# A pooled subtraction in tiles of six rows: the first tile of three rows (2 and 1), the last of five (3, 1 and 1)

## The chip, the cores and the metric

The kernel runs on one core of a Trainium2 chip. The metric is the device time of one execution in microseconds (us); the time of a kernel is the median of its runs. The profile comes from one further execution, in which the hardware profiler recorded instructions and DMA packets.

## The reference

The input `x` is a float32 tensor of shape (8, 64, 256, 256), 134.22 MB. Each 256x256 image is cut into windows of 8x8. The maximum of each window is taken, spread back over its window, and subtracted from the input:

```python
x_r = x.reshape(B, C, oH, 8, oW, 8)
pooled = x_r.max(axis=(3, 5))
upsampled = np.repeat(np.repeat(pooled, 8, axis=2), 8, axis=3)
return x - upsampled
```

The output has the shape and type of the input. Every byte is read once and written once, 268.44 MB in all.

## The kernel before, in words

Eight image lines of 256 values make one "row" of 2048 floats (8 KB), which holds 32 whole windows. There are 16384 such rows. A tile gives each of the 128 partitions R consecutive rows, so a tile of R rows is R MiB. The rows are cut into 22 tiles: tile 0 of `sum(HEAD)` = 4 rows, tiles 1 to 20 of `SIZE` = 6 rows, and tile 21 of `sum(TAIL)` = 4 rows. Together these are 4 + 120 + 4 = 128 rows per partition.

One buffer in SBUF, `ring`, has four slots of six rows each (`SLOTS`, line 15). Tile i lives in slot (i - 1) modulo 4: tiles 1, 2, 3 in slots 0, 1, 2, tile 0 in slot 3, tile 4 in slot 3 again, and so on; tile 21 is in slot 0 with tile 17 before it. The data are changed in place: a tile is loaded into its slot, reduced into `tops`, subtracted in the slot, and stored from there. Nothing is copied.

Three engines' queues share the work, each in an order that is written out by hand:

- SP issues the loads (line 113). Tile 0 is loaded in the pieces of `HEAD`, every other tile in one transfer. Before a load into a slot that was used, SP waits (line 110) until the stores of the tile before it in that slot have landed; so SP issues tiles 0 to 3 at once, and tile 4 waits for both stores of tile 0.
- VectorE does all the arithmetic, in `pool_and_subtract`: one reduce over the whole piece (line 81) and then one subtract for each row (line 96). Tile 0 is handled in the pieces of `HEAD_OUT`, where each piece waits until the load that completes it has landed (line 138). Tiles 1 to 20 run in a hardware loop (line 140); its wait, through the helper `take` on line 75, is for `filled`, which TensorE's queue counts up when a load has landed (line 121). Tile 21 is loaded whole (wait on line 148) and handled in the pieces of `TAIL` (line 149).
- The queue of ScalarE (ACT) issues the stores (line 130), one for each piece that VectorE has finished: the pieces of `HEAD_OUT` for tile 0, one for each of tiles 1 to 20, the pieces of `TAIL` for tile 21. At the end it waits for the last stores to land (line 134).

Loads and stores are two DMA queues on the same 16 DMA engines: q1 carries the loads and q10 the stores. In a transfer of R rows each packet is one partition's R rows, R times 8 KB; 128 packets on 16 engines are eight for each engine.

The sizes are set in these lines:

```python
HEAD, HEAD_OUT = [3, 1], [2, 2]
SIZE, TILES = 6, 20
TAIL = [2, 1, 1]
SLOTS = 4
```

Of the kernel before, what the change touches and what calls it, by code (L numbers as in the profile page):

```python
# [1 line left out]

# [4 lines left out]

F32 = mybir.dt.float32
ROW = 2048


HEAD, HEAD_OUT = [3, 1], [2, 2]
SIZE, TILES = 6, 20
TAIL = [2, 1, 1]
SLOTS = 4


@with_exitstack
def kernel(
    ctx: ExitStack,  # L20
    tc: tile.TileContext,
    x: bass.AP,
    out: bass.AP,
):
    nc = tc.nc
    P = nc.NUM_PARTITIONS
    B, C, H, W = x.shape
    pH = pW = 8
    oW = W // pW

    x_rows = x.rearrange("b c (oh ph) w -> (b c oh) (ph w)", ph=pH)
    out_rows = out.rearrange("b c (oh ph) w -> (b c oh) (ph w)", ph=pH)
    sizes = [sum(HEAD)] + [SIZE] * TILES + [sum(TAIL)]
    assert sum(sizes) * P == x_rows.shape[0] and max(sizes) == SIZE
    starts = [P * sum(sizes[:i]) for i in range(len(sizes))]
    last = len(sizes) - 1

    data = ctx.enter_context(tc.tile_pool(name="data", bufs=1))
    ring = data.tile([P, SLOTS * SIZE * ROW], F32, name="ring")
    tops = data.tile([P, SLOTS * SIZE * oW], F32, name="tops")  # L40
    first = [tc.alloc_semaphore(f"first{i}") for i in range(len(HEAD))]
    loaded = [tc.alloc_semaphore(f"loaded{i}") for i in range(SLOTS)]
    stored = [tc.alloc_semaphore(f"stored{i}") for i in range(SLOTS)]
    final = tc.alloc_semaphore("final")
    filled = tc.alloc_semaphore("filled")
    reduced = tc.alloc_semaphore("reduced")
    pooled = tc.alloc_semaphore("pooled")
    ready = tc.alloc_semaphore("ready")

    def slot_of(i):  # L50

        return (i - 1) % SLOTS

    def dram(rows, i):

        n = sizes[i]
        return rows[starts[i] : starts[i] + P * n].rearrange("(p r) d -> p (r d)", r=n)

    def sbuf(i, lo, R):
        at = (slot_of(i) * SIZE + lo) * ROW  # L60
        return ring[:, at : at + R * ROW]

    def top(i, lo, R):
        at = (slot_of(i) * SIZE + lo) * oW
        return tops[:, at : at + R * oW]

    def cuts(parts):
        lo = 0
        for R in parts:
            yield lo, R  # L70
            lo += R

    def take(sem, n):

        nc.vector.wait_ge(sem, n).then_inc(sem, -n)  # L75

    def pool_and_subtract(part, top, R, nth=None):

        wins = part.rearrange("p (r ph ow pw) -> p r ph ow pw", r=R, ph=pH, ow=oW)
        maxs = top.rearrange("p (r ow) -> p r ow", r=R)  # L80
        nc.vector.tensor_reduce(  # L81
            out=maxs if R > 1 else maxs[:, 0],
            in_=(
                wins.rearrange("p r ph ow pw -> p r ow ph pw")
                if R > 1
                else wins[:, 0].rearrange("p ph ow pw -> p ow ph pw")
            ),
            axis=mybir.AxisListType.XY,
            op=mybir.AluOpType.max,
        ).then_inc(reduced if nth is None else pooled, 1)  # L90
        if nth is None:
            take(reduced, 1)
        else:
            nc.vector.wait_ge(pooled, nth)
        for r in range(R):
            sub = nc.vector.tensor_tensor(  # L96
                out=wins[:, r],
                in0=wins[:, r],
                in1=maxs[:, r].unsqueeze(1).unsqueeze(3).to_broadcast([P, pH, oW, pW]),
                op=mybir.AluOpType.subtract,  # L100
            )
        sub.then_inc(ready, 1)

    with tc.tile_critical(sync_engine=nc.gpsimd.engine, no_gpsimd_drain=True):

        landed = [0] * SLOTS
        for i in range(len(sizes)):
            slot = slot_of(i)
            if landed[slot]:
                nc.sync.wait_ge(stored[slot], 16 * landed[slot])  # L110
            for k, (lo, R) in enumerate(cuts(HEAD if i == 0 else [sizes[i]])):
                part = slice(lo * ROW, (lo + R) * ROW)
                nc.sync.dma_start(out=sbuf(i, lo, R), in_=dram(x_rows, i)[:, part]).then_inc(
                    first[k] if i == 0 else loaded[slot], 16
                )
            landed[slot] += len(HEAD_OUT) if i == 0 else 1


        for i in range(1, last):
            turn = (i - 1) // SLOTS + 1  # L120
            nc.tensor.wait_ge(loaded[slot_of(i)], 16 * turn).then_inc(filled, 1)


        done = n_final = 0
        for i in range(len(sizes)):
            for lo, R in cuts(HEAD_OUT if i == 0 else TAIL if i == last else [SIZE]):
                part = slice(lo * ROW, (lo + R) * ROW)
                done += 1
                nc.scalar.wait_ge(ready, done)
                nc.scalar.dma_start(out=dram(out_rows, i)[:, part], in_=sbuf(i, lo, R)).then_inc(  # L130
                    stored[slot_of(i)] if i + SLOTS <= last else final, 16
                )
                n_final += i + SLOTS > last
        nc.scalar.wait_ge(final, 16 * n_final)


        for k, (lo, R) in enumerate(cuts(HEAD_OUT)):
            nc.vector.wait_ge(first[[a + n >= lo + R for a, n in cuts(HEAD)].index(True)], 16)
            pool_and_subtract(sbuf(0, lo, R), top(0, lo, R), R, k + 1)
        with nc.vector.Fori(0, TILES) as i:  # L140
            slot = i % SLOTS
            take(filled, 1)
            pool_and_subtract(
                ring[:, bass.ds(slot * (SIZE * ROW), SIZE * ROW)],
                tops[:, bass.ds(slot * (SIZE * oW), SIZE * oW)],
                SIZE,
            )
        nc.vector.wait_ge(loaded[slot_of(last)], 16 * ((last - 1) // SLOTS + 1))
        for k, (lo, R) in enumerate(cuts(TAIL)):
            pool_and_subtract(sbuf(last, lo, R), top(last, lo, R), R, len(HEAD_OUT) + k + 1)  # L150


# [1 line left out]
_INS = ['x']  # L154
_OUTS = [((8, 64, 256, 256), 'float32')]


# [23 lines left out]
```

## Time and profile before

| what | value |
|---|---|
| median of 5 runs | 626.66 us |
| the 5 runs | 626.46, 629.63, 626.60, 626.69, 626.66 us |
| the profiled execution, its own time | 626.32 us |
| its span, first to last instruction | 624.5 us |
| VectorE busy | 560.2 us (90%) |
| reduce of six rows, x20 | 12.95 us each |
| reduce of two rows, x3; of one row, x2 | 4.42; 2.28 us |
| subtract of one row, x128 | 2.29 us each |
| loads of 6, 4, 3 and 1 MiB, issue to landing | 38.1, 33.3, 9.8, 11.9 us (medians) |
| stores of 6, 2 and 1 MiB, issue to landing | 50.9, 24.6, 13.8 us (medians) |

The span runs from the first to the last instruction of the program; the execution's own time is 1.8 us longer. "Busy" is the time in which an engine computed. The time from the issue of a transfer to its landing includes what it waits behind others on the same DMA engines. In lists of instructions a line has the start, the duration, the engine, the source line, the operation and the tiles written and read; "ACTq" and "SPq" are the queues that issue DMAs. In windows by stage a line has the stretch, its length, the busy time and number of instructions of VectorE and GpSimd, the granted clock of TensorE, the share of the DMA engines' time that was taken, and GB/s. That share can go a little over 1 in a short stretch.

### The profile page before, as it was taken

Reading aid. Unit: us, or ns where it says so; the run is one execution under the profiler, and the core shown is the slowest. Engines: PE = TensorE matmul, PEld = TensorE weight load, DVE = VectorE, ACT = ScalarE, POOL = GpSimd, SP = SyncE. Lnnn points to the kernel's source line nnn. Section 1 sums busy time; section 2 is a strip of 40 time slices with the busy share of each in tenths; the row PEclk is TensorE's granted clock in tenths of the full one; section 3 lists DMA queues with packets and bytes.
Section 4 is the critical chain, followed back from the end, with each engine's and each line's share of the span. In section 5 each row is a group of like instructions: output and inputs, shape, how many; then the busy total and the mean of one; then the engine's idle time right before and its main releaser. Section 6 shows DMA issues by size and latency. Waiting matters only on the chain. (4 is left out here: it accounts for less than half of the span.)

```text
span 624.5 us, 519 instructions
## 1 busy us (share of the span) xinstructions
DVE 560.2 (90%) x153; POOL 0.2 (0%) x4
## 2 busy tenths in 40 slices
DVE  3899999999999898989898989889898989898991
POOL 0000000000000000000000000000000000000000
DMA  9999999999999999999999999999999999999998
GB/s 369 411 438 427 453 403 453 441 416 453 419 438 453 403 453 428 428 453 403 453 438 419 453 416 441 453 403 453 425 431 453 403 453 434 422 453 428 445 403 369
DMA packets 6912, 268.44 MB, mean 430 GB/s; under 512 B 768, under 2 KB 768, under 8 KB 768
## 3 DMA queue, kind: packets, MB, share of 16 engines
q1 hardware_dynamic: 3312, 134.22, 49.9%
q10 hardware_dynamic: 3600, 134.22, 49.7%
HBM read 134.22 MB, written 134.22 MB: 430 GB/s over the span
## 5 line engine op out<-in xcount | busy, mean ns | idle before, releaser
L81 DVE TENSOR_REDUCE tops<-ring (+2 forms) x25 | 276.8, 11073 | 47.2 <-DVEq L75 36.4
L96 DVE TENSOR_TENSOR ring<-ring,tops (+1 forms) x128 | 284.1, 2286 | 3.3 <-DVEq L75 3.1
L165 POOL MEMSET const-bfloat16-1.0<- 128x1 bf16 x1 | 0.1, 101 | 0.0
L165 POOL MEMSET const-uint8-127<- 128x1 uint8 x1 | 0.1, 101 | 0.0
L165 POOL MEMSET const-float32-0.0<- 128x1 f32 x1 | 0.1, 98 | 0.2 <-issue 0.2
L165 POOL MEMSET const-float32-1.0<- 128x1 f32 x1 | 0.1, 98 | 0.0
## 6 DMA issues: line engine op xcount, KB each, us to landing
ring<-in_x_dram SPq DMA_DIRECT2D x20, 6144.0 KB, 38.1
out_dram<-ring ACTq DMA_DIRECT2D x20, 6144.0 KB, 50.9
out_dram<-ring ACTq DMA_DIRECT2D x3, 2048.0 KB, 24.6
ring<-in_x_dram SPq DMA_DIRECT2D x1, 4096.0 KB, 33.3
ring<-in_x_dram SPq DMA_DIRECT2D x1, 3072.0 KB, 9.8
out_dram<-ring ACTq DMA_DIRECT2D x2, 1024.0 KB, 13.8
ring<-in_x_dram SPq DMA_DIRECT2D x1, 1024.0 KB, 11.9
```

The costliest lines, as they stand in the source:

```text
L81: nc.vector.tensor_reduce(out=maxs if R > 1 else maxs[:, 0], in_=(wins.rearrange("p r ph ow pw -> p r ow ph pw") if R > 1 else wins[:, 0]. ...
L96: sub = nc.vector.tensor_tensor(out=wins[:, r], in0=wins[:, r], in1=maxs[:, r].unsqueeze(1).unsqueeze(3).to_broadcast([P, pH, oW, pW]), op ...
L165: nc = _bacc.Bacc("TRN2", target_bir_lowering=False, num_devices=1)
```

## The change

Tile 0 has three rows instead of four. It is loaded as two rows and one instead of three and one, and reduced, subtracted and stored as two and one instead of two and two. Tile 21 has five rows instead of four, is loaded in one transfer as before, and is reduced, subtracted and stored in pieces of three, one and one instead of two, one and one. Tiles 1 to 20 keep their size; each begins 128 rows (1 MiB) earlier in the input and the output. The numbers of loads (23) and of stores (25) stay.

```diff
-HEAD, HEAD_OUT = [3, 1], [2, 2]
+HEAD, HEAD_OUT = [2, 1], [2, 1]
 SIZE, TILES = 6, 20
-TAIL = [2, 1, 1]
+TAIL = [3, 1, 1]
 SLOTS = 4
```

On the engines' queues this means: on SP the first load has 128x4096 elements instead of 128x6144, and the last 128x10240 instead of 128x8192. On VectorE the second reduce covers one row instead of two, with one subtract behind it instead of two; the first reduce of the tail covers three rows instead of two, with three subtracts behind it. On ACT the second store has 128x2048 elements instead of 128x4096, and the first of the last three 128x6144 instead of 128x4096.

## The prediction

> **What bounds the kernel now.** I read the page first, for the engines and the DMA queues.
>
> ```profile
> DVE 560.2 (90%) x153; POOL 0.2 (0%) x4
> q1 hardware_dynamic: 3312, 134.22, 49.9%
> q10 hardware_dynamic: 3600, 134.22, 49.7%
> HBM read 134.22 MB, written 134.22 MB: 430 GB/s over the span
> ```
>
> VectorE is busy 90% of the span. Loads (q1) and stores (q10) together hold the 16 DMA engines for 49.9 + 49.7 = 99.6% of 624.5 us, that is 622.0 us. Only 2.5 us are free of packets, so I asked next where they lie, with the windows by stage.
>
> ```profile
> 0.00:2.00 2.00, 0.00 (x0) 0.20 (x4) 1.00 0.35 86
> 2.00:13.00 11.00, 2.25 (x1) 0.00 (x0) 1.00 1.05 437
> 13.00:30.00 17.00, 15.49 (x6) 0.00 (x0) 1.00 0.97 395
> 190.00:560.00 370.00, 336.91 (x90) 0.00 (x0) 1.00 1.00 434
> 591.00:622.50 31.50, 19.52 (x8) 0.00 (x0) 1.00 0.99 428
> 622.50:624.50 2.00, 0.00 (x0) 0.00 (x0) 1.00 0.07 29
> ```
>
> The last two columns are the DMA share and GB/s. Loads alone (2 to 13 us) run at 437, loads with stores (190 to 560) at 434, stores alone (591 to 622.5) at 428. The direction of the traffic makes almost no difference, and the free time is the first 2 and the last 2 us. So the kernel is a pipe that is full from end to end: one row per partition (1 MiB one way) costs 1.0486 MB / 434 GB/s = 2.42 us wherever it is moved.
>
> The chain of waits must not mislead here. It ends with VectorE's work, because VectorE's last subtract is the last computing instruction; I read the waits and the timeline of the end to see whether anybody waits for VectorE.
>
> ```profile
> DVE tops L81 <- DVEq L75: 36.4, 15, 2.6
> DVE tops L81 <- DMA ring<-in_x_dram: 10.7, 1, 10.7
> SPq L113 <- DMA out_dram<-ring: 547.6, 18, 60.4
> 592.64 4.41 DVE L81 TENSOR_REDUCE tops<-ring 128x64 f32<-128x4096 f32 x1
> 592.76 18.24 ACTq L130 DMA_DIRECT2D out_dram<-ring  x4
> 608.33 2.29 DVE L96 TENSOR_TENSOR ring<-ring,tops 128x2048 f32<-128x2048 f32 x1
> ```
>
> VectorE waits for tiles 2.6 us at a time, late in the run, and SP waits 547.6 us for stores to free a slot. The last of the four stores issued from 592.76 on goes out near 610.7, when VectorE is done, and yet the span ends at 624.5: the line 130 view has 12.7 us as the shortest way of a store to its landing. The packet records say why: the last store's first packet starts at 620.15, when the stores ahead of it are through. Between issue and first packet an unhindered transfer needs 1.0 us (first load, issued 0.88, first packet 1.88), the first store beside loads 3.6 (19.73 to 23.35). So the last issue is covered by 620.15 - 610.66 - 3.6 = 5.9 us at least.
>
> **The bytes and the packets.** The change moves no byte more or less. The program has 23 loads and 25 stores as before. The packets by size: a head load of 24 KB per packet becomes 16 KB, the last load 32 KB becomes 40 KB; a head store of 16 KB becomes 8 KB, the first tail store 16 KB becomes 24 KB. By the packet records (0.31 us for 8 KB, 0.61 for 16, 0.91 for 24, 1.21 for 32, so 1.51 for 40 by the same step) the loads give -0.30 + 0.30 and the stores -0.30 + 0.30 for each of a transfer's eight packets per engine: the sum is 0.0 us. A bound from the windows: the store stretch with its two 1 MiB stores ran 428 against 434, 31.5 x 6/434 = 0.4 us lost. If one more 1 MiB store lost all that, +0.4; if the 3 MiB piece saves it again, -0.4. I take 0, by the packets, which are the nearer row.
>
> Against it the Trainium skill, "DMA: Bandwidth & Descriptors", section on measured bandwidth, gives 341 GB/s for a transfer of 1 MB against 425 for 16 MB (on the GpSimd path, another one than here), and advises larger batches. By that figure, an estimate, the new 1 MiB store costs 0.7 us more than at 434, and the sum would be 627.3. The 428 GB/s above speaks against it: a queue with work behind it hides what a lone transfer shows.
>
> **The head.** The first load is one row shorter: VectorE starts at 10.75 - 2.42 = 8.3. Two rows take 4.42 + 4.50 = 8.9 us as before, so the first store goes out at 19.73 - 2.42 = 17.3. The second piece is now one row, 2.28 + 2.29 = 4.6 us instead of 8.9, and its store goes out near 21.9 instead of 28.59. It gains nothing by that, since it is queued behind the first store. That one is slow: its eight 16 KB packets per engine take turns with 48 KB load packets, 8 x (0.61 + 1.82) = 19.4 us, and the first packets of the two head stores indeed lie 20.3 us apart. With 8 KB packets the second needs 8 x (0.31 + 1.82) = 17.0. So the slot of tile 0 comes free at 63.7 - 2.4 - 2.4 = 58.9, and SP, which is held there by the wait at line 110, issues tile 4 then.
>
> What that sets off: in the stretch where loads bind, slots turn round every 29.0 us, and each load follows a store's landing. All loads and stores of the middle move forward by about 4.8 us. This is not a gain in time: tile 0 has one row fewer and tile 21 one more, and the 4.8 us are that row moved in and out, 2 x 2.42. Until 165 us VectorE is the slower one and the loads only run further ahead; the DMA engines stay full there (434 GB/s from 64 to 190), as slots free earlier, not later. The first 2 us stay: the first packet comes 1.0 us after the first issue for any size.
>
> **The tail.** Tile 20 starts at 566.31 - 4.8 = 561.5 and ends at 587.8. The last load now goes out at 556.73 - 4.8 = 551.9 with 5 MiB; the page has 33.3 us for 4 MiB, plus 2.42 gives 35.7, landing 587.6, just when VectorE asks for it. If the 6 MiB row holds instead (38.1), it lands at 590.0 and VectorE waits 2.2 us. The first piece of three rows: reduce 4.42 + (12.95 - 4.42)/4 = 6.55, subtract 4.50 + 2.2 = 6.7, so 13.3 us against 8.9; its store goes out at 601.2 and nobody on the store queue lacks work, as tile 20's 6 MiB are under way until 613.2. Two one-row pieces of 4.5 follow: VectorE ends at 587.8 + 13.3 + 9.1 = 610.2, against 610.6 before. With the late landing it is 612.4. Both lie within the 5.9 us of cover. The last store is 1 MiB as before and ends the span as before.
>
> **Sum.** 624.5 + 0 (bytes) + 0 (packets) + 0 (head, since it displaces queued work) + 0 (tail, covered) = 624.5; the profiled run is 626.32, so 1.8 us lie outside the span. That run is 0.3 us under the median of 626.66, which the forecast takes over: 626.7.
>
> **Rivals.** *The early start is carried through to the end.* If order and latency set the time, not the full pipe, the first store's 2.4 us or the slot's 4.8 us would be saved: 624.2 or 621.9. For it: loads bind from 190 us on, and they do come earlier. Against it: 99.6% of the DMA engines' time is taken, and with 2.5 us free in all, 4.8 cannot be saved, 2.4 only by moving at no cost at both ends. 4%.
>
> *The tail's end comes out of its cover* (slower). Place: the last store's issue, behind five rows of VectorE's work that cannot begin before 5 MiB have landed. Price: each us by which the issue lies past 610.66 + 5.9 = 616.6 is a us of idle DMA. If the head's 4.8 us did not reach the tail, VectorE would end at 592.64 + 22.4 = 615.0, still covered. If besides the last load took the 6 MiB row's 38.1 us from 556.73, landing 594.8, the end is 617.2 and the kernel 0.6 slower, 627.3. To be slower by over 1.9 us the tail must start 8.3 us later than the 587.8 above; with a whole row's 4.5 us of VectorE exposed the time would be 631.2. 6%, for this or another loss of DMA rate.
>
> *The change does no more than shift the phase.* That is the forecast, 90%. Within it two terms stay open. The window from 13 to 30 us, where stores join the loads, ran 395 against 434, 17 x 39/434 = 1.5 us lost, for a cause the profile does not name. The stores now join earlier. If that loss vanishes, 625.2; if it doubles, 628.2. These ends take in the 0.4 us of the small store, the late load of the second rival and most of the 90%, and I make them the range.
>
> 0.3% of this kernel, about what a measurement of it can tell from no change, is 1.9 us: faster 4%, within 90%, slower 6%.
>
> **What would show it.** Right: both queues again sum to about 99.6%; the first reduce starts near 8.3; SP issues tile 4 near 58.9; the 29.0 us turns in the middle stand, about 4.8 us earlier; VectorE ends near 610 and the span near 624.5. Wrong: a DMA share below 0.95 in any window between 2 and 622 us, above all in the last 30; a last store that lands less than 6 us after its issue; a reduce of the tail that waits for its load by more than 6 us; or a rate in the middle other than 434.

## The result, and the profile after

The changed kernel takes 629.62 us (median of 48 runs, 626.51 to 634.56); the kernel before, run beside it, 626.93 us (median of 90). The ratio is 1.0043, 95% interval 1.0034 to 1.0052: slower by 0.4%, about 2.7 us, and outside the range of the forecast (625.2 to 628.2). Medians here and below are over all runs; the ratios leave out runs of over 1.5% more than the fastest of the same kernel, so that the two can differ, most of all where a kernel's runs scatter widely. The change moves the odds more than every run: 43 of its 48 runs took 629.1 us or more and four 626.5 to 627.8, while of the 90 runs of the kernel before 77 took less than 628 us and six over 629.6. The profiled execution took 629.95 us with a span of 628.2, 3.7 us more than the span before.

The page first, engines and DMA queues of the changed kernel:

```profile
span 628.2 us, 519 instructions
DVE 560.1 (89%) x153; POOL 0.2 (0%) x4
q1 hardware_dynamic: 3312, 134.22, 49.7%
q10 hardware_dynamic: 3600, 134.22, 49.4%
HBM read 134.22 MB, written 134.22 MB: 427 GB/s over the span
```

The two queues hold the engines for 99.1% of 628.2, that is 622.5 us, against 622.0 before. So the packets together cost half a microsecond more, but the time without packets has grown from 2.5 to 5.7 us. The windows by stage say where:

```profile
64.00:190.00 126.00, 125.22 (x36) 0.00 (x0) 1.00 1.00 431
190.00:560.00 370.00, 335.60 (x90) 0.00 (x0) 1.00 1.00 433
591.00:622.50 31.50, 22.54 (x9) 0.00 (x0) 1.00 0.96 415
622.90:626.30 3.40, 0.00 (x0) 0.00 (x0) 1.00 0.13 53
```

The last line is the one to look at. In the kernel before, the same window is empty, and packets ended at 622.97:

```profile
622.90:626.30 3.40, 0.00 (x0) 0.00 (x0) 1.00 0.00 0
```

Now 3.4 us more are worked at a DMA share of 0.13. That is 2/16: two of the 16 engines are still at work and the other 14 have finished. In a window of the middle the same loss can hardly be seen (433 against 434 GB/s).

The packet records allow more. The profile does not name the engine of a packet, but an engine's packets follow one another without a gap, and each transfer gives each engine eight packets and one end mark of 4 bytes, so the records can be strung together to 16 chains. Worked out so, with the "excess" of an engine as the sum of what its packets took over the shortest packet of the same size (after 40 us):

```
                     engines, end of the last packet (us)     excess after 40 us
before               all 16: 622.5 to 623.0                   0.0 to 0.5
the change           14: 622.4 to 622.9; 2: 626.3 and 626.7   0.0 to 0.3; 3.2 and 3.5
```

Fourteen engines end where they ended before. Two have the same bytes and the same packets, but some of their load packets were stretched, and the last packet ends 3.7 us later than before, which is the whole difference of the spans. On the first of them the 48 KB packets (1.815 us otherwise) that start at 172.9, 202.0, 231.1, 260.3, 289.7, 319.5 and 332.9 us take 0.05, 0.10, 0.22, 0.39, 0.62, 0.73 and 0.90 us longer: one in each turn of 29 us or so, the last two 13 us apart, growing, and after 340 us no more than 0.2. Of the 22 packets between 70 and 585 us that were stretched by over 0.05 us, 17 are the first load packet behind the end mark of a store or the first packet of a new load; these two places hold 560 of about 4,560 large packets. Of the 22 only two are stores.

What the forecast had said of the head, of SP and of the tail, in the timeline and the waits of the changed kernel:

```profile
8.30 4.42 DVE L81 TENSOR_REDUCE tops<-ring 128x64 f32<-128x4096 f32 x1 [8.30 <-DMA ring<-in_x_dram]
58.59 0.33 SPq L113 DMA_DIRECT2D ring<-in_x_dram  x1
564.99 12.95 DVE L81 TENSOR_REDUCE tops<-ring  x1 [2.59 <-DVEq L75]
591.32 6.55 DVE L81 TENSOR_REDUCE tops<-ring 128x96 f32<-128x6144 f32 x1
591.43 22.58 ACTq L130 DMA_DIRECT2D out_dram<-ring  x4
597.91 6.69 DVE L96 TENSOR_TENSOR ring<-ring,tops 128x2048 f32<-128x2048 f32 x3
611.36 2.29 DVE L96 TENSOR_TENSOR ring<-ring,tops 128x2048 f32<-128x2048 f32 x1
DVE tops L81 <- DVEq L75: 42.0, 14, 7.0
```

The first reduce and the issue of tile 4 are where they were expected (8.3 and 58.9). Tile 20 begins at 565.0 instead of 561.5: a load has landed only when the slowest engine has its part, and that engine is 3.5 us late by then. VectorE's waits at line 75 grow from 36.4 to 42.0 us, but most of that is not the late engine: 4.6 of the 5.6 us lie ahead of tile 1, which VectorE now reaches earlier (the first wait at line 75, before and then after, stands below); 1.0 us comes later. The tail waits for no load.

```profile
30.95 12.95 DVE L81 TENSOR_REDUCE tops<-ring  x1 [2.40 <-DVEq L75]
28.76 12.95 DVE L81 TENSOR_REDUCE tops<-ring  x1 [6.98 <-DVEq L75]
```

### The profile page after: what moved, and what is told of

It reads as the page before. It is cut to its first block, busy times and chain, and to the rows that moved or that the text cites. A ratio compares the mean times of both kernels' runs of the same rounds, so it can differ in the third digit from the quotient of the medians.

```text
span 628.2 us, 519 instructions
## 1 busy us (share of the span) xinstructions
DVE 560.1 (89%) x153; POOL 0.2 (0%) x4
## 5 line engine op out<-in xcount | busy, mean ns | idle before, releaser
L81 DVE TENSOR_REDUCE tops<-ring (+3 forms) x25 | 276.8, 11073 | 50.3 <-DVEq L75 42.0
## 6 DMA issues: line engine op xcount, KB each, us to landing
out_dram<-ring ACTq DMA_DIRECT2D x20, 6144.0 KB, 48.9
```

The source lines that it names most:

```text
L81: nc.vector.tensor_reduce(out=maxs if R > 1 else maxs[:, 0], in_=(wins.rearrange("p r ph ow pw -> p r ow ph pw") if R > 1 else wins[:, 0]. ...
```

## The experiments

The theory at the start: the 3 us are lost by a few DMA engines, which get out of step with the others where the first stores join the loads; sizes and bytes cost nothing. The rivals: the five-row tail uncovers the end; the sizes or the shifted addresses cost it.

**The tail in other pieces.**

```diff
-TAIL = [3, 1, 1]
+TAIL = [2, 2, 1]
```

> The change with the last tile's five rows in pieces of 2, 2 and 1 instead of 3, 1 and 1. Theory 'out of step': the head is that of the change, so the time is that of the change, 629.5 within 0.3. Theory 'tail': the store of the tail's first piece goes out 4.4 us earlier, and 1 to 3 us of the loss go: 626.6 to 628.6.

629.60 us (6 runs, from 629.45), ratio 1.0051 (1.0033 to 1.0068). The time is that of the change. The windows of this kernel show the same picture, two engines' worth of work after the rest is done:

```profile
623.00:626.00 3.00, 0.00 (x0) 0.00 (x0) 1.00 0.12 49
```

The share of 0.12 is two engines of 16. So the three-row piece is not what costs. The rival "tail" falls for its pieces; its five rows come below.

**The early first load alone**, on the kernel before:

```diff
-HEAD, HEAD_OUT = [3, 1], [2, 2]
+HEAD, HEAD_OUT = [2, 2], [2, 2]
```

> The first load has two rows as in the change, tile 0 keeps four rows (loaded 2 and 2, stored 2 and 2) and the tail its 2, 1, 1. Theory 'out of step' (the extra 3 us of the changed kernel are lost by two DMA engines that fall out of step with the other fourteen when the first stores join the loads, and the sizes themselves cost nothing): the joining is 2.4 us earlier as in the change, so its time may be anywhere between 626.5 and 629.7, and the slowest DMA engine's end in the packet records must account for the whole difference. Theory 'tail' (five rows behind tile 20 uncover the end): 626.6, as before.

629.29 us, but in groups: five of 12 runs between 625.9 and 627.0, five between 629.2 and 629.6, two above 632. Ratio 1.0020 (0.9996 to 1.0043), not clear. Its profile came from a run of 629.42 us and has a DMA share of 0.18 from 623 to 626 us, three engines of 16:

```profile
623.00:626.00 3.00, 0.00 (x0) 0.00 (x0) 1.00 0.18 76
```

With tile 0 and the tail at four rows, the loss of the change appears in about half of the runs.

**A delay of 0.95 us before the first store**, sizes untouched, on both kernels (the tile `spare`, a semaphore and some arguments are left out here):

```diff
+nc.vector.memset(spare[:, :], 0.0)
 for k, (lo, R) in enumerate(cuts(HEAD_OUT)):
     nc.vector.wait_ge(first[...], 16)
+    if k == 0:
+        nc.vector.tensor_reduce(out=spare_max, in_=spare, ...)   # 832 elements, 1.02 us
```

> The change with a dummy reduce of about 0.95 us on VectorE ahead of the first reduce, so that both head stores go out about half a 48 KB packet (1.82 us) later. Theory 'out of step': the moment at which the first stores join decides which engines fall out of step, so the time changes by more than the 0.95 us can explain, most likely back to 626.5 to 627.5; it stays at 629.5 if the moment does not matter. Theory 'tail': 629.5, as in the change. Were the start of VectorE on the path, it would be 630.4.

> The kernel before with the same dummy reduce of about 0.95 us ahead of its first reduce. Theory 'out of step': it may come to 629.5, if the moment of the joining decides, and the extra time then sits in a few DMA engines alone; at 626.7 the moment alone is not what decides. Theory 'tail': 626.7, as the tail is untouched. Were the start on the path: 627.6.

The change with the delay: 628.10 us (11 runs), ratio 1.0031 (1.0010 to 1.0053). The kernel before with the delay: 630.14 us (6 runs, from 628.44), ratio 1.0047 (1.0030 to 1.0065). The second is slower by three times the delay, clear of noise. The first is 1.5 us faster in the median than without the delay, but the intervals of the two ratios overlap, so this is not shown. (Its first store went out at 18.67 us for 17.29, since its first load landed 0.5 us later, too; in the kernel before at 20.68 for 19.73.) In the packet chains of the kernel before with the delay 13 engines end between 622.2 and 622.9, the latest at 625.9 with 3.8 us of excess; its windows:

```profile
591.00:622.00 31.00, 20.29 (x9) 0.00 (x0) 1.00 0.97 417
623.00:626.00 3.00, 0.00 (x0) 0.00 (x0) 1.00 0.09 38
```

So the loss of the changed kernel can be had with the sizes of the kernel before. The first condition I formed from these traces: before, half of the engines load while the other half store, in the others nearly all go in the same direction (at 300 us, 8 of 16 engines load before, 15 in the change, 16 in the kernel before with the delay); the loss belongs to the latter ("in step").

**Eight engines moved out of step by hand.** On SP's queue ahead of tile 8's load, a DMA that reaches eight engines only, with two tiny packets and an end mark (three turns), or with one and an end mark (two turns, the control; semaphores are left out here):

```diff
+if i == NUDGE_AT:   # 8
+    few = lambda t: t.rearrange("p (a b) -> p a b", a=2)[:, :NUDGE, :128]   # NUDGE: 2 or 1
+    nc.sync.dma_start(out=few(nudge[:8, :]), in_=few(x_rows[:8, :512]))
```

> The changed kernel, and on SP's queue, ahead of the load of tile 8 (near 175 us), one extra DMA of 8 partitions with two pieces of 512 bytes each, so that eight of the 16 engines get two tiny load packets and an end mark, three turns, and from there on load while the others store. Theory 'in step' (time is lost at the change from one transfer to the next on single engines when nearly all engines load and store at the same moments, and not when about half do the opposite): the losses after 180 us go, the slowest engine ends near 623.5, time 626.5 to 627.5. Rival 'head timing' (the engines that lose are fixed in the head): 629.5.

> The control: the same extra DMA with one piece of 512 bytes for each of 8 partitions, so that the eight engines get one tiny packet and an end mark, two turns, and stay in the same step as the others. Theory 'in step': losses as in the changed kernel, 629.5 (629 to 633). If the tiny DMA by itself, by whatever disturbance, took the loss away, this one too would come to 626.5.

> The kernel before with the 0.95 us dummy reduce, which ran in step and took 630.1, with the extra DMA of three turns on eight engines ahead of tile 8's load. Theory 'in step': 627 to 628 (what was lost before 175 us stays, up to 0.6 us). Rival 'head timing': 630.

> The control of it, with two turns: by the theory 'in step' 629 to 631, as without the extra DMA; by the rival the same.

Measured: 636.65, 636.83, 636.94 and 635.47 us; ratios 1.0131 (1.0092 to 1.0170), 1.0061 (1.0028 to 1.0093), 1.0134 (1.0097 to 1.0170) and 1.0117 (1.0087 to 1.0147). The prediction of "in step" fails outright: three turns were to heal and made it worse by 7 us, and three of the four kernels lose 3 us or more on every engine (the DMA queues of the first are busy 49.8% and 48.9% of a span of 635.8, and most of its engines end near 630.7). The second kernel's runs lie anywhere between 626.5 and 641.1 us, and its interval overlaps that of the change, so a cost of its extra DMA is not shown. What the other three do show: less than 10 KB more traffic costs 5 to 7 us in the median against the same kernel without it, and in their profiles each engine has 3.4 to 12 us of stretched packets, most of it in loads.

**SP's moment of issue.** The second condition: a change of packet near SP's issue of a load is stretched. On the kernel before, SP was held after each wait for a slot by a chain of waits on a semaphore of its own:

```diff
-nc.sync.wait_ge(stored[slot], 16 * landed[slot])
+nc.sync.wait_ge(stored[slot], 16 * landed[slot]).then_inc(tick, 1)
+for _ in range(LATE):   # 6, 12 or 24
+    ticks += 1
+    nc.sync.wait_ge(tick, ticks).then_inc(tick, 1)
+ticks += 1
```

> The kernel before; after each wait for a free slot SP spends about 0.5 us more (a chain of six waits on a semaphore of its own) before it issues the load. Theory 'issue window' (an engine loses time when its change from one packet to the next falls close to the moment at which SP issues a load; in the kernel before all changes lie about 1.0 to 0.3 us before or 0.8 to 1.6 us after it): the changes now fall up to 0.5 us nearer on one side, so some engines lose: 627 to 630, extra time in single engines. Rival 'spread alone' (what counts is how the engines stand to each other, not SP's moment): 626.6, since the load queue holds some 9 us of work when SP issues.

> The same with twelve waits, about 0.9 us, half a 48 KB packet: by the issue window nearly all changes of packet meet SP's issue, so most engines lose and the time is the worst of the three, 629 or more. Rival: 626.6.

> The same with 24 waits, about 1.8 us, one whole 48 KB packet: by the issue window the moment lies as before in the packets' rhythm, 626.5 to 627.5. Rival: 626.6.

> The kernel before unchanged, for a second profile. Both theories: span near 624.5, all 16 engines through with their packets between 622.4 and 623.0, and about half of them loading while the others store; if its time is 2 us or more over 626.5, a few engines must be late by that.

From the last mark of a store to SP's issue it took 0.02 us before, and now mostly 0.49, 0.89 and 1.69. Times: 627.60 (ratio 0.9999, 0.9985 to 1.0014), 628.59 (1.0010, 0.9996 to 1.0024) and 629.59 us (1.0030, 1.0014 to 1.0046), beside 627.59 of the kernel before; the fastest runs 627.05, 627.60 and 628.84 against 626.37. The kernel before again: 626.56 us, all 16 engines through between 622.4 and 623.2. SP's moment does count, by 2 us at the far end; the two shorter delays are not clear of noise. It counts though the load queue has work in hand when SP issues: in the kernel before SP issues at 92.66 us, and the load then under way ends between 99.1 and 101.5 on the 16 engines. But the window that I had named is wrong: at 0.89 us hardly a packet in the middle was stretched, and at a whole packet, where the loss was to vanish, it was greatest. With six waits all 16 engines lose about 1.7 us alike and none falls behind; here the DMA share from 623 to 626 us is 0.47:

```profile
623.00:626.00 3.00, 0.00 (x0) 0.00 (x0) 1.00 0.47 199
```

**Delays by whole packets, and other addresses.** The third condition ("collapse"): in the change the engines end the head's second store from 56.5 us on and begin tile 1's store from 58.7 on, and in this gap eight engines fit in two loads and eight one, after which 14 engines stood alike; before, every engine fits in one and the groups of 8 and 8 stay. The dummy reduce was set to 1664 elements, once or twice, for one or two packets of 1.8 us. In the fourth kernel the rows are dealt out in another order:

```diff
-starts = [P * sum(sizes[:i]) for i in range(len(sizes))]
+order = [*range(1, last), 0, last]
+starts = [P * sum(sizes[j] for j in order[: order.index(i)]) for i in range(len(sizes))]
```

> The change with its first reduce 1.81 us later, one whole 48 KB packet, so that the stores join the loads at the same point of a packet as in the change (10 engines one load earlier than the other 6), while the head's second store ends one packet later. Theory 'collapse' (in the kernel before about half of the engines run one turn behind the rest and nothing is lost; in the change the store queue runs dry for some 2 us before tile 1's store, some engines load twice in that gap, and 14 engines fall into one step): the gap closes, each engine loads once in it, two groups of about 10 and 6 stay, no packets are stretched after 70 us, time 626.5 to 627.5. Rival 'sizes or addresses' (the 3 us come with the sizes): 629.5. Rival 'any delay shifts the odds': between them, without the two groups.

> The same with 3.6 us, two whole packets, the gap surely closed. Theory 'collapse': two groups kept, 626.5 to 627.5. Rivals: 629.5, or 630.4 if the later end of the head's stores costs by itself.

> The kernel before with 1.81 us ahead of the first reduce, where 0.95 us brought all 16 engines into one step at the joining and 630 us. Theory 'collapse': a whole packet leaves the joining as in the kernel before, 8 and 8 within two or three engines, 626.5 to 627.5. Rival 'delay costs by itself': 630 or more.

> The change with the same sizes and order of work, but other rows: tiles 1 to 20 take the rows from 0 on, tile 0 the three behind them, tile 21 the last five. Theory 'collapse': addresses do not matter, 629.5 as the change. Rival 'addresses' (moving all tiles by 1 MiB costs the 3 us): 626.6.

- One packet on the change: 631.04 us, six of 12 runs from 626.5 to 628.6 and six from 633.5 to 637.7; ratio 1.0033 (0.9996 to 1.0069). Not clear; its profile is of one of the long runs, 636.17 us, and is not used.
- Two packets on the change: 627.39 us (626.66 to 629.39) beside 627.37 of the kernel before, ratio 0.9999 (0.9982 to 1.0016). All engines end between 622.3 and 623.3. The loss is gone, with all the sizes and addresses of the change.
- One packet on the kernel before: 628.08 us (626.12 to 633.35), ratio 1.0015 (0.9988 to 1.0043): not clear.
- Other addresses: 630.14 us (from 629.39), ratio 1.0048 (1.0027 to 1.0068), as the change. Other addresses cost the same, so it is not the move of the tiles by 1 MiB that costs.

The page and the windows of the kernel with two packets of delay read like those of the kernel before:

```profile
q1 hardware_dynamic: 3312, 134.22, 49.9%
q10 hardware_dynamic: 3600, 134.22, 49.7%
623.00:626.00 3.00, 0.00 (x0) 0.00 (x0) 1.00 0.00 0
```

Yet its engines stand in no two groups of like size (at 300 us, 14 of 16 load, where it was 8 before), so its good time doesn't come from where "collapse" had it.

**The change without its early start, and with a store queue that does not run dry.**

```diff
-HEAD, HEAD_OUT = [2, 1], [2, 1]
+HEAD, HEAD_OUT = [3], [2, 1]          # head_3
+HEAD, HEAD_OUT = [2, 1], [1, 1, 1]    # head_111
```

> The change without its earlier start: tile 0 has three rows but is loaded in one transfer, so VectorE begins near 10.8 and the first store goes out near 19.8 us as in the kernel before; stored 2 and 1, the tail 3, 1 and 1. Theory 'timing' (the 3 us depend on when the stores join the loads, not on the sizes): the joining is that of the kernel before, 626.5 to 627.7, with all DMA engines through near 623. If the five-row tail or the three-row tile 0 cost it: 629.5.

> The change with tile 0 stored in three pieces of one row: the first store goes out near 12.9 us, and the three stores of 17 us each keep the store queue busy past the moment at which tile 1's store comes, so the queue does not run dry. By the theory 'timing' the time may be anywhere between 626.5 and 633, and the lateness of the slowest DMA engine must account for all of it; by 'collapse' (the dry store queue is what does the harm) 626.5 to 627.5; by 'sizes' 629.5.

The first: 627.10 us (626.69 to 628.51, 11 runs) beside 627.16, ratio 1.0001 (0.9992 to 1.0010). Tile 0 of three rows, the tail of five in pieces of 3, 1 and 1, and all addresses are those of the change; what is undone is the split of the first load, and with it the start of VectorE and the first store, which go out as in the kernel before:

```profile
10.96 4.42 DVE L81 TENSOR_REDUCE tops<-ring 128x64 f32<-128x4096 f32 x1 [10.96 <-DMA ring<-in_x_dram]
19.94 34.29 ACTq L130 DMA_DIRECT2D out_dram<-ring  x3
587.54 6.54 DVE L81 TENSOR_REDUCE tops<-ring 128x96 f32<-128x6144 f32 x1
600.73 2.28 DVE L81 TENSOR_REDUCE tops<-ring 128x32 f32<-128x2048 f32 x1
```

(Its profile is from a run of 627.88 us, one of its longer ones; six engines are late by 1 to 2 us in it.) Here the tail starts at 587.5, where the forecast had it at 587.8, and the time is within 0.4 us of the forecast's. The second kernel: 634.24 us (627.74 to 639.32, nine runs), ratio 1.0088 (1.0058 to 1.0117). By the packet records the head's last store is under way until 61.3 to 62.5 us, and each engine goes from it straight to tile 1's store; the store queue is not dry, and the loss is the greater. "Collapse" falls with it.

## Why the prediction was wrong

- **What bounds the kernel**: right as far as it went. Both kernels are full of packets from 2 to 622 us.
- **Bytes and packets, 0 us**: right. A packet of 8, 16, 24 or 48 KB takes at its shortest 0.31, 0.61, 0.91 and 1.815 us in both traces, and 40 KB 1.514, the forecast's 1.51. The 0.7 us that would follow, as an estimate, from the rates of the Trainium skill ("DMA: Bandwidth & Descriptors", measured bandwidth) for the third 1 MiB store is not seen: 14 engines that move these stores end at 622.4 to 622.9, as before.
- **The head**: the times were right (8.30 for 8.3, 17.29 for 17.3, 21.81 for 21.9, 58.59 for 58.9). Its price, "0 (head, since it displaces queued work)", is the step that failed. With the first load in one piece the change costs nothing (1.0001), with it split 1.0043; split, but with the first store 3.8 us later, again nothing (0.9999). So the term that was put at 0, head and first store 2.4 us earlier, measured +2.7 us.
- **The tail**: right. Three rows took 13.2 us for 13.3; the last store went out 13.3 us before it landed, so the cover that was worked out held (in the packet chains the last store of the kernel before starts at 620.01, not 620.15, which makes it 5.75 us instead of 5.9). The five rows and their pieces are free, as head_3 shows.
- **How the step failed**: the forecast read "99.6% busy" as one pipe, whose order of packets does not matter. There are 16 engines, each with the same eight packets of every transfer, and 14 of them stood idle from 622.9 us on while two worked until 626.7. The Trainium skill says that the engines of a transfer finish independently ("DMA: Bandwidth & Descriptors", section on why a DMA increments its semaphore by 16); the trace agrees, the last load's 16 marks arriving between 585.2 and 591.3 us, and between 587.7 and 590.0 before. A mean over 16 engines hides two that are 3.5 us late: it moved by half a microsecond.
- **The rivals**: the early start was not carried to the end, and the tail did not come out of its cover. "Another loss of DMA rate", put into the 6% without a mechanism, is nearest to what happened. The 1.5 us left open where stores join the loads (13 to 30 us) shrank, 411 for 395 GB/s, and was no help. A spread of the kernel before was in sight as well, a run of 629.63 beside four of 626.5 to 626.7; I took it for noise, and it should have widened the range upwards.

Shown is, then, that in the profiled run of the change, whose time is near the median, the loss lies in stretched packets, nearly all loads, of two engines; that it depends on when the transfers of the head are under way; and that sizes, addresses and tail cost nothing by themselves. Not shown is why a packet is stretched; that cause stays open. Three conditions (engines in step, changes of packet near SP's issue, a dry store queue) each fitted the traces they were formed on and failed the next test. Nor is it a matter of later being better: first stores issued at 17.3, 18.7, 19.4 and 21.1 us gave 629.6, 628.1, 631.0 and 627.4 in the change, and 19.7, 20.7 and 21.6 gave 626.9, 630.1 and 628.1 in the kernel before (medians; with 18.7, 19.4 and 21.6 the runs scatter over more than 6 us).

## What to carry to other kernels

Where the DMA queues are full from end to end, a mean busy share says little on the last engine: look at the share in the last few microseconds (0.13 is two engines of 16), and at how far apart the marks of one transfer arrive. A forecast of "no change" for such a kernel holds for bytes and packets, but here a shift of the first transfers by 1 to 4 us moved it by 0.4 to 0.5%, up or down; keep that in the range. And when a resized tile costs time, try the timing without the size (a dummy delay) and the size without the timing, as head_3 does, before the size is blamed.

## What the runs showed of the hardware that was not expected

- With equal bytes and packets, single DMA engines ended 3 to 4 us after the others, by load packets that took up to 0.9 us longer than 1.815 us, 17 of 22 stretched packets where one transfer follows another.
- One DMA of eight partitions with two pieces of 512 bytes each, in the middle of a run of 268 MB, raised the time from 629.6 to 636.7 us in the median (runs from 630.3 to 639.4).
- SP's issue of each load 1.7 us later, with work left in the load queue (6 to 9 us of it in the kernel before), made the kernel slower by 0.3% (1.0014 to 1.0046); with 0.5 and 0.9 us later no difference is clear of noise.
